# YOCO trunk, one core: four classical chunks at each half step's entry, mixing in three steps, a written order at the recurrence's end, squares moved to other engines

## Chip, cores and metric

One NeuronCore of a Trainium2 chip runs the whole program in one launch. The metric is device microseconds (us) of an execution; the lower the better. Traces come from the hardware profiler.

## The reference, cut to what matters

512 tokens, width 1024, two layers, everything in float32. Each layer does a half-step SwiGLU, a token mixer, a second half-step SwiGLU and a gated input embedding (PLE); layer 0 mixes by an HGRN2 gated linear recurrence, layer 1 by latent attention (MLA).

```python
def _rmsnorm(x, g):
    x32 = x.astype(jnp.float32)
    y = x32 * lax.rsqrt(jnp.mean(x32 * x32, axis=-1, keepdims=True) + EPS)
    return (y * g.astype(jnp.float32)).astype(x.dtype)

def _swiglu(h, w_in, w_out):
    gate, up = jnp.split(h @ w_in, 2, axis=-1)
    return (jax.nn.silu(gate) * up) @ w_out
...
    for li in range(DEPTH):
        g = norm_gains[li]
        x = x + 0.5 * _swiglu(_rmsnorm(x, g[0]), ffn_w_in[li, 0], ffn_w_out[li, 0])
        h = _rmsnorm(x, g[1])
        ...
        x = x + 0.5 * _swiglu(_rmsnorm(x, g[2]), ffn_w_in[li, 1], ffn_w_out[li, 1])
        gate = jax.nn.sigmoid((_rmsnorm(x, g[3]) @ ple_w_gate[li]).astype(jnp.float32))
        x = x + (gate * (p[li] @ ple_w_in[li]).astype(jnp.float32)).astype(x.dtype)
```

There are thus four half steps, called here FFN0 to FFN3, with a hidden width of 2816, that is 22 chunks of 128.

## The kernel before, in words

The residual stays on chip, transposed: eight tiles `x[m]` of 128 features by 512 tokens. Every operand of a product is split into a high and a low part (`split`: ACT rounds, DVE subtracts), and each product is three matmuls: high*high, high*low, low*high. Weights come in tiles of 128x1024 (512 KB), loaded by SP; a tile is *cut* into `whi` (ACT) and `wlo` (DVE) before PE can use it.

A half step (`ffn`) treats its 22 chunks in groups of 6, 8 and 8. The first two chunks (`PLAIN`) are *classical*: gate and up each take one weight tile and 24 matmuls of 512 columns. The other chunks go in *pairs* by Strassen's scheme: seven products of 24 matmuls of 256 columns replace eight. A pair needs sums of weight tiles (one made by a DMA that adds, issued by POOL, others by DVE) and sums of activations. The latter are made at the entry by `mix`, for each of four pairs of `x` tiles: ACT scales two tiles (`be`, `bo`), DVE makes two halves of `ta`, POOL two halves of `tb`, and `ta` and `tb` are split. A pair's first product needs none of them, the second `ta` and the third `tb` of all four. After each group, `outward` multiplies by the second weight matrix; `post` then splits the finished `x[m]` for what follows and adds its square to a running sum (`Stats`), ACT squaring and POOL adding, the last one added by DVE.

The half step runs in *slots*, one weight tile each: `work(t)` issues the load of a later tile, cuts tile t+2 and sums tile t+3; `at(dt, fn, late)` files other work in front of that or behind it. Inside `manual_schedule` the engines named keep the written order; elsewhere a planner orders every engine's instructions from its own estimates. In `plain` the four classical slots each hold one whole `mix` (line 398). FFN0 differs: its first two chunks are computed while `x` is still arriving (`primed`, lines 1163 to 1205, in an order written out for SP and PE), and its four `mix` calls stand before the slots, in the planner's hands.

The recurrence (`hgrn`) goes over four pairs of heads. `recur` is a generator with ten stretches: dots of q and k (line 204), three steps of score matmuls (line 706) whose results DVE copies under masks into `D` (line 716) while DVE and POOL scale q and k, then smaller products, the product with v, a norm and a spread. The planner fills PE meanwhile with independent chains: for the last pair the gates of heads 4 to 7 and the first half of the output projection (`project(0)`). `project(1)` needs the last two heads.

Of the kernel before, what the change touches and what calls it, by code (L numbers as in the profile page):

```python
# [21 lines left out]
DFF = 2816  # L22
NF = DFF // P
GROUPS = [(0, 6), (6, 14), (14, 22)]
PLAIN = 2
HT = T // 2
A_HEADS = 8
B_HEADS = 16
# [28 lines left out]
def kernel(  # L57
# [56 lines left out]
    def soon(n):  # L114
        return tc.high_priority(offset=n)
# [57 lines left out]


    class Stats:
        def __init__(self, n):
            self.n, self.acc, self.seen = n, None, 0
# [65 lines left out]

    ONE, TWO = slice(0, HT), slice(HT, T)

    def mix(nx, i, res):
        col, xg = nx.cols[0], nx.xg[0]
        be, bo = slot("be", F32, "r"), slot("bo", F32, "r")
        for b, m in ((be, 2 * i), (bo, 2 * i + 1)):
            act.activation(b, x[m], AF.Copy, scale=gain(col, m))  # L250
        ta, tb = slot("ta", F32, "r"), slot("tb", F32, "r")
        dve.tensor_tensor(out=ta[:, ONE], in0=be[:, ONE], in1=be[:, TWO], op=ALU.subtract)
        dve.tensor_tensor(out=ta[:, TWO], in0=bo[:, TWO], in1=be[:, TWO], op=ALU.subtract)
        pool.tensor_tensor(out=tb[:, ONE], in0=ta[:, TWO], in1=be[:, ONE], op=ALU.add)
        pool.tensor_tensor(out=tb[:, TWO], in0=tb[:, ONE], in1=bo[:, ONE], op=ALU.subtract)  # L255
        sa, sb = split(ta), split(tb)
        e, o = xg[2 * i], xg[2 * i + 1]
        res.append([
            tuple(a[:, t] for a in part)
            for part, t in ((e, ONE), (sa, ONE), (sb, ONE), (o, ONE), (sa, TWO), (o, TWO), (sb, TWO))  # L260
        ])

    class Weight:

# [42 lines left out]
    def ffn(nx, post, rb=None, primed=(), aside=None, ready=None):  # L307
# [3 lines left out]
        for lo, hi in GROUPS:  # L311
            for f in range(lo, hi):
                if f < PLAIN:
                    if not primed:
# [68 lines left out]
            act.copy(p[0], g)  # L383
            low(p, g)

        def plain():
            xg = nx.xg[0]

            def chain_of(w):
                ps = mm_bank()  # L390
                full(ps, w, xg, range(KC), True, True)
                return ps

            def mixing(i):
                mix(nx, i, b)

            at(0, lambda: mixing(0), True)
            p0 = chain_of(turn())
            sums = nx.stats.sums()
            r = nx.stats.columns(sums)  # L400
            now[0] += 1
            at(0, lambda: mixing(1), True)
            p1 = chain_of(turn())
            pb = spread(r)
            now[0] += 1

            def first_gate():
                st["rb"] = slot("rb", F32, "b")
                act.copy(st["rb"], pb)
                st["g"] = gated(p0)  # L410

            at(0, first_gate)
            at(0, lambda: kept(p1, st["g"]), True)
            if ready is not None:
                at(0, lambda: ready(st["rb"]), True)
            at(0, lambda: mixing(2), True)
            p2 = chain_of(turn())
            now[0] += 1

            def second_gate():  # L420
                st["g"] = gated(p2)

            at(0, second_gate)
            at(0, lambda: mixing(3), True)
            p3 = chain_of(turn())
            now[0] += 1
            at(0, lambda: kept(p3, st["g"]))

        def pair(last):
            g = qpool.tile([P, 2 * T], F32, tag="qq", bufs=2, name=name("g"))  # L430
# [106 lines left out]
            hidden.clear()  # L537

        if primed:
            for i in range(KC // 2):  # L540
                mix(nx, i, b)
            for f in range(PLAIN):
# [4 lines left out]
        with tc.manual_schedule(engines=ALL):  # L547
            for lo, hi in GROUPS:
                fs = range(lo, hi)
                if lo == 0 and not primed:  # L550
                    plain()
# [11 lines left out]
        stream["n"] = (stream["tiles"] - 2) * WB  # L563

    class Next:
        def __init__(self, cols, stats=True):
            self.cols = cols
            self.xg = [[] for _ in cols]
            self.stats = Stats(KC)

        def __call__(self, m):
            for i, col in enumerate(self.cols):
                self.xg[i].append(split(x[m], gain(col, m)))
            self.stats.add(x[m])

    def gcol(layer, i):
        return V_GAIN + (layer * 4 + i) * KC
# [18 lines left out]
    def hgrn(xg, stats, lower, upper, post):  # L596
# [75 lines left out]
        def recur(res, f, k, q, decay, v):  # L672
# [124 lines left out]
            dve.tensor_tensor(out=o1, in0=o1, in1=spread(r), op=ALU.mult)  # L797
            res.append(o1)

        def gate(h):  # L800
            pg = chain(xg)
# [9 lines left out]
            )  # L811
            outs[h] = split(o1, None, "o")

        def project(half):
            for m in range(KC):
                po = chain(outs[4 * half : 4 * half + 4])
                with soon(EV_OFF):
                    dve.tensor_tensor(out=x[m], in0=po, in1=x[m], op=ALU.add)
                    if half == 1:
                        post(m)  # L820

        pairs = A_HEADS // 2
        vals = values(0)
# [2 lines left out]
        for p in range(pairs):  # L826
            res = [[], []]
            live = [recur(res[e], *fkq[e], vals[e]) for e in range(2)]
            while live:
                live = [g for g in live if next(g, live) is not live]  # L830
            if p < pairs - 1:
                vals = values(p + 1)
                fkq = [keys(2 * p + 2 + e) for e in range(2)]
# [4 lines left out]
            if p == pairs - 1:  # L838
                sg = [gate(2 * p + e) for e in range(2)]
                project(0)  # L840
                for e in range(2):
                    finish(2 * p + e, *res[e], sg[e])
        project(1)


    def embed(layer):
# [313 lines left out]
            project(B_HEADS // 2 - 1, part)  # L1160


    first = Next([gcol(0, 0)])
    primed, heads = [mm_bank() for _ in range(4)], []

    def prime(c, *ks):
        for k in ks:
            w = tuple(a[:, k * P : (k + 1) * P] for a in heads[c])
            mm3(primed[c], w, first.xg[0][k], k == 0, k == KC - 1)

    def head(pieces=1):
        fetch(pieces)
        heads.append(stream["ready"].pop(0))
        stream["n"] += WB

    with tc.manual_schedule(engines={mybir.EngineType.SP, mybir.EngineType.PE}):
        nc.sync.dma_start(vc, vec)
        load(0)
        first(0)
        head(4)  # L1180
        prime(0, 0)
        for m in range(1, KC):
            load(m)
            first(m)
            if m == 2:
                head(2)
                prime(0, 1, 2)
                prime(1, 0, 1, 2)
            if m == 4:
                head(2)  # L1190
                for c in range(2):
                    prime(c, 3, 4)
                prime(2, *range(5))
            if m == 5:
# [5 lines left out]
        sums = first.stats.sums()  # L1200
        for c in range(3):
            prime(c, KC - 1)
        head()
# [205 lines left out]
```

## Time and profile before

| | |
|---|---|
| median of three runs | 2227.64 us (2226.56 to 2228.78) |
| the profiled execution | 2227.43 us, of which the span from first to last instruction is 2225.7 us |
| PE busy | 2170.2 us (98%) |
| DVE busy | 1567.6 us (70%) |
| ACT, POOL busy | 986.5 us (44%), 368.0 us (17%) |
| mean granted clock of TensorE | 0.985 of 2.4 GHz |

Matmuls overlap, so that a row's mean duration is longer than the distance from one matmul to the next; distances are read from elapsed time over counts. PEld is the weight load in front of each matmul.

### The profile page before, as it was taken

To read this page: it belongs to the slowest core of one execution; us is meant where nothing else is said; L and a number is where in the kernel's file an instruction comes from. 1 tells how busy PE (TensorE), PEld (TensorE's weight loads), DVE (VectorE), ACT (ScalarE), POOL (GpSimd) and SP (SyncE) were. 2 spreads that over 40 slices of the span, in tenths; PEclk is the share of its full clock that TensorE was granted. 3 is DMA by queue.
4 is the path that set the end of the run, shared out by engine and by line. 5 is a ranking of instruction groups with operands and counts; after the bars stand their busy time and mean duration, and the time that the engine had idled before them with its cause. 6 is when DMAs were issued, how large, how long until landed. Compare 5 with 4: busy or idle time off the path is not lost.

```text
span 2225.7 us, 33449 instructions
## 1 busy us (share of the span) xinstructions
PE 2170.2 (98%) x13314; PEld 1949.5 (88%) x13314; DVE 1567.6 (70%) x2270; ACT 986.5 (44%) x1393; POOL 368.0 (17%) x463
## 2 busy tenths in 40 slices
PE   7999999999998999999989999999999989999998
PEld 6899998889877899998878989988888868999987
DVE  7777676778777676676767757767677776775765
ACT  6344353322335443354553434446454554343543
POOL 3000001555433000001110000022111130000011
PEclk9999999999998999999989999999999989999999
DMA  5555552211123565552334655423122215664631
GB/s 181 163 152 161 141 163 99 79 64 67 67 71 90 152 156 160 150 155 101 104 95 133 180 151 144 152 85 105 60 84 86 67 58 151 160 167 129 179 105 48
DMA packets 77836, 267.80 MB, mean 120 GB/s; under 512 B 9328, under 2 KB 11504, under 8 KB 77680
## 3 DMA queue, kind: packets, MB, share of 16 engines
q1 hardware_dynamic: 65296, 222.25, 29.9%
q0 software_dynamic: 11520, 41.95, 11.2%
q8 instruction: 105, 1.72, 0.3%
q10 hardware_dynamic: 864, 1.46, 0.2%
q14 instruction: 51, 0.42, 0.1%
HBM read 259.33 MB, written 2.10 MB: 117 GB/s over the span
## 4 chain that ended last, share of the span: by engine, by line
PE 88%; DVE 4%; issue 4%; ACT 2%; POOL 1%; DMA 0%; POOLq 0%; DVEq 0%; SPq 0%; ACTq 0%
PE aux L301 20%; PE mm L301 15%; PE mm L151 15%; PE mm L150 15%; PE mm L152 15%; PE aux L706 1%; PE aux L151 1%; PE aux L152 1%; PE aux L150 1%; DVE wlo L292 1%; PE aux L1116 1%; POOL tb L255 1%; PE aux L1090 0%; PE aux L1091 0%; DVE wlo L129 0%
## 5 line engine op out<-in xcount | busy, mean ns | idle before, releaser
L151 PE MATMUL mm<-lo,whi 128*128 128x512 f32 x1544 | 609.4, 395 | 10.0 <-DVE lo L169 8.8
L150 PE MATMUL mm<-hi,whi 128*128 128x512 f32 x1544 | 604.3, 395 | 12.6 <-ACT whi L128 6.8
L152 PE MATMUL mm<-hi,wlo 128*128 128x512 f32 x1544 | 605.3, 392 | 0.5 <-DVE wlo L129 0.5
L292 DVE TENSOR_TENSOR wlo<-raw,whi 128x1024 fp32r<-128x1024 f32 x348 | 439.8, 1264 | 204.0 <-ACT whi L291 200.6
L291 ACT CAST whi<-raw 128x1024 fp32r<-128x1024 f32 x348 | 363.4, 1045 | 287.1 <-PE mm L151 151.2
L301 PE MATMUL aux<-hi,whi 128*128 128x256 f32 x1280 | 370.7, 290 | 12.7 <-ACT whi L291 5.3
L301 PE MATMUL aux<-lo,whi 128*128 128x256 f32 x1280 | 368.4, 288 | 4.5 <-DVE lo L166 4.5
L301 PE MATMUL aux<-hi,wlo 128*128 128x256 f32 x1280 | 368.3, 288 | 2.3 <-DVE wlo L292 2.0
L151 PEld LDWEIGHTS mm<-lo,whi 128*128 128x128 f32 x1544 | 292.1, 189 | 74.3 <-DVE lo L169 14.9
L150 PEld LDWEIGHTS mm<-hi,whi 128*128 128x128 f32 x1544 | 291.7, 189 | 73.8 <-ACT whi L128 6.8
L152 PEld LDWEIGHTS mm<-hi,wlo 128*128 128x128 f32 x1544 | 292.2, 189 | 59.0 <-DVE wlo L129 0.9
L301 PE MATMUL mm<-hi,whi 128*128 128x256 f32 x960 | 271.7, 283 | 0.0
L301 PE MATMUL mm<-lo,whi 128*128 128x256 f32 x960 | 271.7, 283 | 0.0
L301 PE MATMUL mm<-hi,wlo 128*128 128x256 f32 x960 | 271.6, 283 | 0.0
L301 PEld LDWEIGHTS aux<-hi,whi 128*128 128x128 f32 x1280 | 250.9, 196 | 15.5 <-ACT whi L291 6.0
L301 PEld LDWEIGHTS aux<-lo,whi 128*128 128x128 f32 x1280 | 251.3, 196 | 6.2 <-DVE lo L166 5.8
L301 PEld LDWEIGHTS aux<-hi,wlo 128*128 128x128 f32 x1280 | 251.0, 196 | 3.8 <-DVE wlo L292 2.7
L275 POOL DMA_DIRECT2D raw<-in_wall x80 | 69.7, 872 | 976.5 <-DMA raw<-in_wall 423.1
L301 PEld LDWEIGHTS mm<-hi,whi 128*128 128x128 f32 x960 | 184.4, 192 | 0.0
L301 PEld LDWEIGHTS mm<-lo,whi 128*128 128x128 f32 x960 | 184.4, 192 | 0.0
L301 PEld LDWEIGHTS mm<-hi,wlo 128*128 128x128 f32 x960 | 184.3, 192 | 0.0
L128 ACT CAST whi<-raw 128x1024 fp32r<-128x1024 f32 (+2 forms) x104 | 104.3, 1008 | 178.3 <-PE mm L151 131.6
(242 smaller groups left out, 2938.7 us busy)
## 6 DMA issues: line engine op xcount, KB each, us to landing
raw<-in_wall SPq DMA_DIRECT2D x407, 512.0 KB, 3.6
raw<-in_wall POOLq DMA_DIRECT2D x80, 512.0 KB, 6.2
x<-in_xT SPq DMA_DIRECT2D x8, 256.0 KB, 5.7
qr<-hi SPq DMA_DIRECT2D x32, 64.0 KB, 2.0
qr<-lo SPq DMA_DIRECT2D x32, 64.0 KB, 2.0
out_dram<-o SPq DMA_DIRECT2D x8, 256.0 KB, 2.4
p<-in_pT ACTq DMA_DIRECT2D x4, 256.0 KB, 5.1
cs<-in_cst SPq DMA_DIRECT2D x1, 385.0 KB, 7.1
```

The costliest lines, as they stand in the source:

```text
L128: act.copy(hi[:, s], raw[:, s])
L150: pe.matmul(out, a[0], b[0], start=first, stop=False)
L151: pe.matmul(out, a[0], b[1], start=False, stop=False)
L152: pe.matmul(out, a[1], b[0], start=False, stop=last)
L255: pool.tensor_tensor(out=tb[:, TWO], in0=tb[:, ONE], in1=bo[:, ONE], op=ALU.subtract)
L275: nc.gpsimd.dma_start(self.raw, wall[self.plus], accum_op=ALU.add)
L291: act.copy(hi, self.raw)
L292: dve.tensor_tensor(out=lo, in0=self.raw, in1=hi.bitcast(F32), op=ALU.subtract)
L301: pe.matmul(o, w[u][:, s], b[i][v], start=first and e + i + n == 0, stop=False, skip_group_check=True)
L706: pe.matmul(sc[:, e * 192 : (e + 1) * 192].rearrange("p (i b n) -> p i b n", i=2, n=3 * m), k[:, j * P : (j + 1) * P], q4[:, :, j * nbt : ...
L1116: pe.transpose(banks[b][:, o : o + P], prob[i][:, j * P : (j + 1) * P], ident)
```

## The change

`PLAIN` becomes 4: chunks 2 and 3 are now classical in every half step, which takes one pair from each. `mix` becomes a class with three steps: `scale` (ACT), `combine` (DVE, POOL) and `cut` (the splits). In FFN1 to FFN3 `plain` has eight slots: for tile pair i, `scale` in slot max(2i-1, 0), `combine` in slot 2i, `cut` in slot 2i+1. In FFN0 the two primed chunks stay, and four classical slots follow that hold one step of each kind.

At the recurrence's end, PE's order is written: after each stretch of each of the last two heads, `fill` steps (of three matmuls) of a generator that holds gates 4 to 7 and the first half of the projection. FFN0's sum of squares is made by PE (fp32 matmuls with a column of ones) in place of POOL and of the transposes; the sums in front of FFN1 and FFN3 are added by DVE in place of POOL.

```diff
-PLAIN = 2
+PLAIN = 4
+FILL = (3, 4, 3, 3, 3, 3, 3, 2, 2, 3)
...
-                eng = dve if self.seen == self.n else pool
+                eng = dve if self.seen == self.n else self.eng
...
+    class Mix:
+        def scale(self):
+            col = self.nx.cols[0]
+            self.be, self.bo = slot("be", F32, "r"), slot("bo", F32, "r")
+            for b, m in ((self.be, 2 * self.i), (self.bo, 2 * self.i + 1)):
+                act.activation(b, x[m], AF.Copy, scale=gain(col, m))
+        def combine(self):
...
+            dve.tensor_tensor(out=ta[:, TWO], in0=bo[:, TWO], in1=be[:, TWO], op=ALU.subtract)
+            dve.tensor_tensor(out=ta[:, ONE], in0=be[:, ONE], in1=be[:, TWO], op=ALU.subtract)
+            pool.tensor_tensor(out=tb[:, ONE], in0=ta[:, TWO], in1=be[:, ONE], op=ALU.add)
+            pool.tensor_tensor(out=tb[:, TWO], in0=tb[:, ONE], in1=bo[:, ONE], op=ALU.subtract)
+        def cut(self, res):
+            sa, sb = split(self.ta), split(self.tb)
...
+        def plain(f0):
+            mixed = [Mix(nx, i) for i in range(KC // 2)]
+            n = 2 * (PLAIN - f0)
+            if f0:
+                for i in range(KC // 2):
+                    if i == 0:
+                        mixed[0].scale()
+                        mixed[0].combine()
+                        mixed[0].cut(b)
+                        mixed[1].scale()
+                    else:
+                        at(i - 1, mixed[i].combine)
+                        at(i, lambda i=i: mixed[i].cut(b), True)
+                        if i < KC // 2 - 1:
+                            at(i - 1, mixed[i + 1].scale, True)
+            else:
+                for i in range(KC // 2):
+                    at(max(2 * i - 1, 0), mixed[i].scale, i > 0)
+                    at(2 * i, mixed[i].combine, i == 0)
+                    at(2 * i + 1, lambda i=i: mixed[i].cut(b), True)
...
+                ps[t] = aux_bank() if f0 and t < 2 else mm_bank()
+                full(ps[t], w, xg, range(KC), True, True)
...
+        def closing(done, sg):
+            last = 2 * (pairs - 1)
+            for e in range(4):
+                g = gated((yield from steps(xg)))
+                if e < 2:
+                    finish(last - 2 + e, *done[e], g)
+                else:
+                    sg.append(g)
+            for m in range(KC):
+                po = yield from steps(outs[0:4])
...
+        with tc.manual_schedule(engines={mybir.EngineType.PE}):
+            sg = []
+            rest = closing(done, sg)
+            for fill in FILL:
+                for g in live:
+                    next(g, None)
+                    for _ in range(fill):
+                        next(rest, None)
...
-    first = Next([gcol(0, 0)])
+    first = Next([gcol(0, 0)], None)
+    def square(m):
+        sq = slot("sq", F32, "r")
+        act.activation(sq, x[m], AF.Square)
+        for j in range(NT):
+            pe.matmul(
+                dots[:, j : j + 1], sq[:, j * P : (j + 1) * P], ones, start=m + j == 0, stop=m == KC - 1,
...
-    n2 = Next([gcol(0, 2)])
+    n2 = Next([gcol(0, 2)], dve)
-    n6 = Next([gcol(1, 2)])
+    n6 = Next([gcol(1, 2)], dve)
```

## Rows read from the trace of the kernel before

**Rows 1.** The page: busy time by engine, and the chain that ended last by engine.
```profile
PE 2170.2 (98%) x13314; PEld 1949.5 (88%) x13314; DVE 1567.6 (70%) x2270; ACT 986.5 (44%) x1393; POOL 368.0 (17%) x463
...
PE 88%; DVE 4%; issue 4%; ACT 2%; POOL 1%; DMA 0%; POOLq 0%; DVEq 0%; SPq 0%; ACTq 0%
```
**Rows 2.** Busy time by stretch: first the second pair of FFN0, then the first pair of FFN0 (without the two matmuls that ran ahead), FFN1, FFN2 and FFN3. Columns: stretch, its length, PE, PEld, DVE, ACT and POOL busy (with counts), granted clock, DMA share, GB/s.
```profile
64.62:84.83 20.21, 20.21 (x170) 20.21 (x169) 15.74 (x17) 10.72 (x14) 0.00 (x0) 1.00 0.49 159
38.00:64.62 26.62, 22.74 (x168) 22.34 (x167) 20.89 (x26) 14.87 (x19) 4.07 (x5) 0.87 0.55 143
698.70:729.17 30.47, 25.22 (x170) 23.75 (x168) 18.69 (x22) 14.71 (x19) 4.44 (x5) 0.83 0.47 122
1127.84:1159.89 32.05, 25.81 (x169) 24.15 (x168) 20.06 (x25) 15.32 (x20) 5.28 (x6) 0.79 0.46 114
1826.21:1854.87 28.66, 24.50 (x170) 23.25 (x169) 18.26 (x21) 14.10 (x19) 3.47 (x4) 0.88 0.49 129
```
**Rows 3.** The same view: two classical slots of FFN2 (48 matmuls of 512 columns), and four slots of an outward product (96 of them).
```profile
1116.83:1127.84 11.01, 11.01 (x51) 9.10 (x50) 6.95 (x9) 5.83 (x8) 2.27 (x3) 1.00 0.38 88
1011.95:1033.71 21.76, 21.76 (x98) 18.02 (x97) 14.98 (x17) 9.88 (x14) 5.17 (x4) 1.00 0.29 98
```
**Rows 4.** PE's waits from 1110 to 1152 us (FFN2's entry): who waited for what, us in total, times, longest.
```profile
PE aux L301 <- ACT whi L291: 3.7, 1, 3.7
...
PE aux L221 <- POOL t L197: 1.1, 1, 1.1
```
**Rows 5.** Timeline of FFN2's entry around its third `mix` (matmuls left out): start, duration, engine, line.
```profile
1125.63 0.72 ACT L250 ACTIVATE be<-x,vc 128x512 f32<-128x512 f32 x1
...
1128.16 0.42 DVE L252 TENSOR_TENSOR ta<-be 128x256 f32<-128x256 f32 x1
...
1128.99 0.74 POOL L254 TENSOR_TENSOR tb<-ta,be 128x256 f32<-128x256 f32 x1 [9.81 <-DVE ta L253]
...
1129.81 1.08 POOL L255 TENSOR_TENSOR tb<-tb,bo 128x256 f32<-128x256 f32 x1
1130.92 0.62 ACT L165 CAST hi<-tb 128x512 fp32r<-128x512 f32 x1 [1.36 <-POOL tb L255]
1131.57 0.69 DVE L166 TENSOR_TENSOR lo<-tb,hi 128x512 fp32r<-128x512 f32 x1 [1.28 <-ACT hi L165]
...
1133.50 1.03 ACT L291 CAST whi<-raw 128x1024 fp32r<-128x1024 f32 x1
...
1134.56 1.23 DVE L292 TENSOR_TENSOR wlo<-raw,whi 128x1024 fp32r<-128x1024 f32 x1 [1.69 <-ACT whi L291]
```
**Rows 6.** Busy time by stretch at the recurrence's end (columns as in rows 2): before the last pair's dots, from there to the second half of the projection, and the part with the three score steps.
```profile
576.70:597.90 21.20, 21.20 (x109) 17.84 (x108) 13.90 (x21) 7.79 (x13) 6.51 (x7) 1.00 0.21 75
597.90:654.40 56.50, 53.42 (x286) 45.71 (x284) 44.82 (x104) 14.12 (x23) 17.15 (x27) 1.00 0.22 66
599.00:626.00 27.00, 27.00 (x137) 23.48 (x138) 25.57 (x69) 5.39 (x6) 8.06 (x12) 1.00 0.17 59
```
**Rows 7.** Timeline, single instructions there: q*k of the last pair on POOL, its dots on PE, and PE's start on the second half of the projection.
```profile
580.75 2.59 POOL L674 TENSOR_TENSOR D<-q,k 128x512 f32<-128x512 f32 x2 [0.61 <-PE aux L151]
...
597.92 1.84 PE L204 MATMUL aux<-ones,D 128*128 128x1 f32 x16
...
654.39 1.20 PE L150 MATMUL mm<-hi,whi 128*128 128x512 f32 x4 [1.30 <-ACT hi L165]
```
**Rows 8.** Groups by line there: PE's score matmuls from 597.9 to 650 us, DVE's masked copies and residual additions from 599 to 626 us. Columns: count, busy us, mean ns, idle before.
```profile
L706 PE MATMUL aux<-qq,k 128*128 128x192 f32 x48 | 8.9, 327 | 0.0
...
L716 DVE COPY_PREDICATED D<-mk,aux 128x192 f32<-128x192 int32 (+2 forms) x36 | 10.6, 354 | 1.1 <-PE aux L706 1.0
...
L818 DVE TENSOR_TENSOR x<-mm,x 128x512 f32<-128x512 f32 x4 | 2.7, 683 | 0.0
```
**Rows 9.** The start: busy time of 6.85 to 32.2 us (columns as in rows 2), and single instructions in it.
```profile
6.85:32.20 25.35, 22.10 (x80) 15.69 (x81) 18.87 (x24) 16.57 (x30) 13.03 (x11) 0.93 0.64 224
...
12.31 3.05 POOL L187 TENSOR_TENSOR sq<-sq,sq 128x512 f32<-128x512 f32 x2 [0.34 <-ACT sq L182]
...
14.14 3.46 DVE L169 SCALAR_TENSOR_TENSOR lo<-x,vc,hi 128x512 fp32r<-128x512 f32 x2
...
15.96 0.50 PE L151 MATMUL mm<-lo,whi 128*128 128x512 f32 x1 [1.28 <-DVE lo L169]
```
**Rows 10.** Busy time by stretch (columns as in rows 2) where the mixers hand over: 60 matmuls of 512 columns and four transposes, from the last head of MLA to the end of FFN3's first chain; and 96 matmuls, from the second half of the recurrence's projection to the end of FFN1's first chain.
```profile
1785.32:1809.28 23.96, 18.90 (x64) 13.48 (x65) 21.11 (x24) 14.66 (x23) 12.60 (x8) 0.79 0.14 44
654.39:680.07 25.68, 23.58 (x96) 17.80 (x97) 22.47 (x26) 15.17 (x23) 9.89 (x6) 0.99 0.20 67
```
**Rows 11.** Groups by line from 1789 to 1803 us (columns as in rows 8), and, from the timeline, one split of `x` and one addition of squares on DVE at moments when POOL adds nothing.
```profile
L187 POOL TENSOR_TENSOR sq<-sq,sq 128x512 f32<-128x512 f32 x6 | 10.4, 1740 | 18.5 <-ACT sq L182 18.2
...
L169 DVE SCALAR_TENSOR_TENSOR lo<-x,vc,hi 128x512 fp32r<-128x512 f32 x5 | 5.6, 1120 | 0.0
...
L292 DVE TENSOR_TENSOR wlo<-raw,whi 128x1024 fp32r<-128x1024 f32 x2 | 4.0, 1976 | 0.0
...
L252 DVE TENSOR_TENSOR ta<-be 128x256 f32<-128x256 f32 x1 | 1.5, 1498 | 0.0
...
1789.43 0.74 DVE L169 SCALAR_TENSOR_TENSOR lo<-x,vc,hi 128x512 fp32r<-128x512 f32 x1
...
679.11 0.68 DVE L187 TENSOR_TENSOR sq<-sq,sq 128x512 f32<-128x512 f32 x1
```

More of the change, by code (lines that the diff above doesn't have):

```diff
@@ L244, with __init__ @@
     ONE, TWO = slice(0, HT), slice(HT, T)
[L246 to L261, printed above, removed]
+    class Mix:
+        def __init__(self, nx, i):
+            self.nx, self.i = nx, i
+        def scale(self):
[4 more added lines that the diff above has]
+        def combine(self):
+            be, bo = self.be, self.bo
+            ta, tb = self.ta, self.tb = slot("ta", F32, "r"), slot("tb", F32, "r")
+            dve.tensor_tensor(out=ta[:, TWO], in0=bo[:, TWO], in1=be[:, TWO], op=ALU.subtract)
[4 more added lines that the diff above has]
+            sa, sb = split(self.ta), split(self.tb)
+            xg = self.nx.xg[0]
+            e, o = xg[2 * self.i], xg[2 * self.i + 1]
+            res.append([
+                tuple(a[:, t] for a in part)
+                for part, t in ((e, ONE), (sa, ONE), (sb, ONE), (o, ONE), (sa, TWO), (o, TWO), (sb, TWO))
+            ])
     class Weight:
@@ L384, in kept, with fresh @@
             low(p, g)
-        def plain():
+        def plain(f0):
             xg = nx.xg[0]
[L389 to L407, printed above, removed]
+            mixed = [Mix(nx, i) for i in range(KC // 2)]
[17 more added lines that the diff above has]
+                    at(2 * i + 1, lambda i=i: mixed[i].cut(b), True)
+            ps = [None] * n
+            r = pb = None
+            def fresh():
@@ L424, in plain @@
[L424 to L427, printed above, removed]
+            for t in range(n):
+                f = f0 + t // 2
+                if t == 2 and not f0:
+                    at(0, fresh)
+                if t % 2 == 0 and t > 0:
+                    at(0, lambda t=t: st.update(g=gated(ps[t - 2])))
+                    at(0, lambda t=t: kept(ps[t - 1], st["g"]), True)
+                if t == 2 and not f0 and ready is not None:
+                    at(0, lambda: ready(st["rb"]), True)
+                w = turn()
+                ps[t] = aux_bank() if f0 and t < 2 else mm_bank()
+                full(ps[t], w, xg, range(KC), True, True)
+                if t == 0 and not f0:
+                    r = nx.stats.columns(nx.stats.sums())
+                if t == 1 and not f0:
+                    pb = spread(r)
+                now[0] += 1
@@ L539, in ffn @@
         if primed:
-            for i in range(KC // 2):
-                mix(nx, i, b)
-            for f in range(PLAIN):
+            for f in range(len(primed) // 2):
                 kept(primed[2 * f + 1], gated(primed[2 * f]))
@@ L549, in ffn @@
                 fs = range(lo, hi)
-                if lo == 0 and not primed:
-                    plain()
+                if lo == 0:
+                    plain(len(primed) // 2)
                 for f in fs:
@@ L798, in recur, with steps, gated @@
             res.append(o1)
+        def steps(rhs):
+            ps = mm_bank()
+            for k in range(len(rhs)):
+                mm3(ps, block(), rhs[k], k == 0, k == len(rhs) - 1)
+                yield
+            return ps
+        def closing(done, sg):
[8 more added lines that the diff above has]
+                po = yield from steps(outs[0:4])
+                with soon(EV_OFF):
+                    dve.tensor_tensor(out=x[m], in0=po, in1=x[m], op=ALU.add)
         def gate(h):
-            pg = chain(xg)
+            return gated(chain(xg))
+        def gated(pg):
             with soon(EV_OFF):
@@ L828, in hgrn @@
             live = [recur(res[e], *fkq[e], vals[e]) for e in range(2)]
+            if p == pairs - 1:
+                break
             while live:
                 live = [g for g in live if next(g, live) is not live]
-            if p < pairs - 1:
-                vals = values(p + 1)
-                fkq = [keys(2 * p + 2 + e) for e in range(2)]
+            vals = values(p + 1)
+            fkq = [keys(2 * p + 2 + e) for e in range(2)]
             if done is not None:
@@ L837, in hgrn @@
             done = res
[L838 to L843, printed above, removed]
+        with tc.manual_schedule(engines={mybir.EngineType.PE}):
[6 more added lines that the diff above has]
+                        next(rest, None)
+            for _ in rest:
+                pass
+            for e in range(2):
+                finish(2 * p + e, *res[e], sg[e])
+            project()
     def embed(layer):
@@ L1176 @@
     with tc.manual_schedule(engines={mybir.EngineType.SP, mybir.EngineType.PE}):
+        dots = aux_bank()
         nc.sync.dma_start(vc, vec)
@@ L1184 @@
             first(m)
+            if m == 1:
+                square(1)
             if m == 2:
@@ L1193 @@
                 prime(2, *range(5))
+            if m in (2, 4):
+                for k in (m - 1, m) if m == 4 else (m,):
+                    square(k)
             if m == 5:
@@ L1199 @@
                         prime(c, m)
-        sums = first.stats.sums()
+                square(m)
+        sums = dots[:, 0:NT]
         for c in range(3):
```

36 lines of the change are left out of this document (15 added, 21 removed).

## The prediction

> **What bounds the kernel now.** I read the page first. PE is busy 98% of the span and carries 88% of the chain that ended last [rows 1], so time can go in two ways alone: PE gets less to do, or it stands less and keeps its clock. Busy shares hide the second, since a matmul at half clock counts as busy. So next I read busy time by stretch, with elapsed time over the number of matmuls. A quiet pair takes 20.21 us at granted clock 1.00; the first pair of each half step takes 26.62, 30.47, 32.05 and 28.66 us at clock 0.87, 0.83, 0.79 and 0.88, a mean between the two levels of 2.4 and 1.2 GHz [rows 2]. That is the largest loss in the trace: 6.4 + 10.3 + 11.8 + 8.5 = 37.0 us. Of FFN2's, the waits name a weight cut (ACT whi), 3.7 us [rows 4], but the timeline shows that ACT is only the last in a queue: one `mix` walks from ACT (1125.63) over DVE (1128.16), POOL (1128.99 to 1130.89), ACT (1130.92) to DVE (1131.57), each engine standing for the other, and the cut filed behind it comes at 1133.50 [rows 5]. From `be` to the last split are 6.6 us, a classical slot lasts 5.5 [rows 3], so four whole mixes cannot fit four slots, and the pair's second and third product need them all.
>
> **The change part by part.**
>
> *Classical chunks.* Four slots of 24 matmuls take 21.76 us [rows 3]; the pair they replace takes 20.21 [rows 2]. Four half steps: 4 x 1.55 = +6.2 us. This is certain, since PE is the bound.
>
> *Mixing over eight slots.* Work per tile pair does not change, but has 43.5 us in place of 21.8. More than that, no engine meets its own half-made `mix`: `combine` waits for a `scale` filed a slot earlier, `cut` for a `combine` filed a slot earlier, and 5.5 us exceeds every such step (POOL's two additions end 2.7 us after DVE began [rows 5]). What is late next would be the gating of the last classical chunk in front of the first pair; it holds one weight cut of 1.03 + 1.23 us [rows 5], while the products that need that cut lie two slots ahead. FFN0 has four slots, but its first mix stands in front of them and each step again has a slot to itself; in those 21.8 us DVE has four cuts and what is left of four mixes, where it was busy 20.89 of 26.62 us before [rows 2]. I take the loss of the first pairs as gone up to 0.5 us each: -37.0 + 2 = -35.0 us. Bounds: -37.0, and -17 if half the queue remains. In FFN2 PE also waits 1.1 us for the norm's power on POOL [rows 4], behind the whole first mix; with its splits moved out I take -1 (bounds -1.1 and 0).
>
> *Written order at the recurrence's end.* Nothing is added or removed on PE. From the dots to the second half of the projection PE stands 56.50 - 53.42 = 3.1 us [rows 6], 1.3 of it at the end for the last split [rows 7]; the written order keeps nine steps of filling (9 x 3 x 0.227 = 6.1 us) behind the last spread, so these 3.1 go. Against it: gates can no longer run ahead of the dots. Before, PE had no idle time from 576.7 to 597.9 [rows 6], while POOL made the last pair's q*k only from 580.75 on, done by 583.3 [rows 7]; in the written order PE may stand for it, between 0 and 583.3 - 576.7 = 6.6 us. The pair before still has its own products in that time, so I take 0.6. And DVE: the three score steps hold 25.57 us of DVE work [rows 6]; PE is now given 20 filling steps there, 13.6 us, and the score matmuls, 8.9 us at most [rows 8], 22.5 together. DVE's residual additions, 2.7 us [rows 8], move out, since the gates now come first: 25.57 - 2.7 - 22.5 = 0.4 us; with both steps not overlapping well I take 1.5. Sum -3.1 + 0.6 + 1.5 = -1 us; bounds -3.1 and +8 (the 6.6, 3.5 of DVE and a little clock).
>
> *Squares of FFN0 on PE.* 32 dots make 64 matmul records; 16 take 1.84 us [rows 7], so +7.4 us of PE. Part falls where PE stands: 3.25 us of the first 25.35, at clock 0.93 [rows 9]. And POOL's additions go: two splits of `x` beside them took 3.46 us [rows 9] against 0.74 each alone [rows 11], and PE waited for just these at 15.96 [rows 9]. I take +2; bounds -2 (stalls and half clock gone as well) and +7.4 (no cover).
>
> *Squares in front of FFN1 and FFN3 on DVE.* At both places DVE is PE's releaser and is busy 21 to 22 of 24 to 26 us; PE loses there 23.96 - 60 x 0.227 - 0.4 = 9.9 and 25.68 - 96 x 0.227 = 3.9 us [rows 10]. Six additions of 0.68 put 4.1 us on DVE per place. What it gets back is read from the same stretch: beside POOL's six additions a split takes 1.12 in place of 0.74 (five: 1.9 us), a weight cut 1.98 in place of 1.23 (two: 1.5), and half a `ta` 1.50 in place of 0.42 (1.1) [rows 5, 11]; 4.5 us. So nearly even: I take -1 for both places, bounds +8.2 (nothing given back) and -10 (rival B).
>
> The Trainium skill (SBUF — State Buffer, section "Who interferes with whom") says that a DVE instruction with two SBUF inputs and a GpSimd instruction that reads SBUF exclude each other for a whole instruction. The stretched splits and cuts agree with it [rows 11]. By that rule POOL's six additions close the port for their own length, and the exchange gives more than even: that is rival B, whose price below stands on rows.
>
> The sum: +6.2 - 35.0 - 1 - 1 + 2 - 1 = -29.8 us on the profiled execution's 2227.43, which lies 0.2 under the median: **2197.6 us**.
>
> **The rivals.**
>
> *A. The written order starves PE mildly.* DVE's work in the score steps does not shrink and q*k comes late: +8 in place of -1, so 2206.6. For it: DVE at 25.57 of 27 us [rows 6]. Against: before, that load lay beside 27 us without idle time on PE, and half the region has little for DVE.
>
> *B. DVE is freed at the handovers.* POOL's six additions last 10.4 us in FFN3's handover [rows 11]; if DVE's work on two operands may lie beside none of them, 10.4 us come free for 4.1 paid, 6.3, and at FFN1's handover all of the 3.9 that PE loses there: -10 in place of -1, so 2188.6. For it: splits are what PE waits for. Against: the additions now stand in DVE's own queue in front of the next split.
>
> *C. Half the first pairs' loss stays,* since the queue in front of the pair is also gating and weight cuts: +18, so 2215.6. For it: the wait names whi [rows 4]. Against: second pairs, with as many cuts, lose nothing [rows 2].
>
> *D, the other side.* The written order serialises PE and DVE: at each of the 20 places PE waits for the head's whole share. A head's score step is 25.57 / 6 = 4.3 us of DVE; six of them are 25.6 us, the other 14 places at the 1.3 us of the last split [rows 7] 18 more, and with PE working half the time the clock falls as in FFN2's first pair, which costs its region another 20% (15 us). Together +59, against -29 for the rest: about 2258. It decides from 30 us lost in that region, that is, when PE stands a third of it. For it: PE's queue is fixed, and one late DVE copy holds everything behind it. Against: the fill between two stretches of one head (4.1 to 5.4 us and the other head's matmuls) is longer than 4.3 us.
>
> **How the numbers follow.** Chances: my forecast (2190 to 2204) 0.52, A 0.18, B 0.16, C 0.08, D 0.04, and 0.02 for a disorder of the planner elsewhere. The range goes from B's far end to C's: 2182 to 2214 us. A measurement of this kernel can tell 0.2%, 4.5 us, from no change; faster means below 2223. Forecast, A, B and C lie there; with a little taken off for several mishaps at once: faster 0.93, same 0.02, slower 0.05.
>
> **What would show it.** First pairs at 20 to 21 us and clock 1.00 in all four half steps prove the mixing; a wait of PE in the first pair on anything from `Mix` refutes it. Eight slots at 43.5 us prove the price of the classical chunks. Recurrence: PE's idle time between the last pair's dots and the projection under 3 us, and DVE near full in the score steps. Start: FFN0's first slot about 2 us later than prime's end at 38.0 was before. Handovers: splits of `x` back at 0.74 us, and PE's loss in the two stretches of rows 10 near 13 us in all; near 5 would be B. I am wrong if the sum comes right by other terms, or if the first pairs are clean and the time is still above 2214.

## The result and the profile after

The changed kernel takes 2199.58 us (median of four, 2199.11 to 2200.0), the kernel before on the same chip 2227.29; the ratio is 0.9875, 95% interval 0.9858 to 0.9892. The prediction was 2197.6. The sum came out, but two of its terms were wrong by 7 and by 4 us, in opposite directions, so that it came within 2 us is in part luck. One execution of a kernel below (`e2_gates_first`) took 12208 us, with every matmul more than five times as long, and is left out.

The page after, the lines of [rows 1]:

```profile
PE 2166.1 (99%) x13086; PEld 1938.7 (88%) x13086; DVE 1522.0 (69%) x2252; ACT 968.6 (44%) x1373; POOL 330.0 (15%) x437
...
PE 94%; DVE 3%; issue 1%; ACT 1%; DMA 0%; POOL 0%; POOLq 0%; SPq 0%; DVEq 0%; ACTq 0%
```

PE's share of the chain rose from 88 to 94%: it still bounds the kernel and stands less. Busy time by stretch (columns as in [rows 2]): from the start to FFN0's first slot, FFN0's four slots, the first pairs of FFN0 to FFN3, and the eight slots of FFN1, FFN2 and FFN3.

```profile
6.85:41.00 34.15, 34.15 (x164) 29.32 (x165) 15.26 (x24) 18.15 (x31) 3.10 (x4) 1.00 0.58 201
41.00:62.78 21.78, 21.78 (x98) 18.02 (x97) 18.84 (x27) 13.85 (x22) 7.92 (x8) 1.00 0.36 96
62.78:82.93 20.15, 20.15 (x170) 20.15 (x168) 12.83 (x14) 10.80 (x13) 0.00 (x0) 1.00 0.46 153
722.76:742.91 20.15, 20.15 (x169) 20.14 (x168) 12.38 (x13) 10.72 (x13) 0.00 (x0) 1.00 0.44 141
1141.60:1161.75 20.15, 20.15 (x169) 20.15 (x168) 12.38 (x13) 10.73 (x13) 0.00 (x0) 1.00 0.44 143
1826.57:1846.73 20.16, 20.16 (x170) 20.15 (x169) 12.38 (x13) 10.74 (x13) 0.00 (x0) 1.00 0.41 143
...
679.22:722.76 43.54, 43.54 (x197) 36.03 (x196) 28.51 (x41) 24.06 (x35) 9.94 (x11) 1.00 0.37 103
1098.06:1141.60 43.54, 43.54 (x197) 36.04 (x196) 28.42 (x42) 22.86 (x34) 9.00 (x11) 1.00 0.37 104
1783.03:1826.57 43.54, 41.91 (x181) 34.24 (x182) 27.63 (x39) 20.56 (x30) 10.46 (x11) 0.96 0.37 104
```

All four first pairs last 20.15 us at clock 1.00, where [rows 2] had 26.62 to 32.05. FFN3's slots are cut as the last 43.54 us before its pair; the last of the handover's stall lies in that stretch.

The rest of the time is read from the *ways* between half steps: from the last pair of one to the first pair of the next, less the classical slots at their own length (21.76 before, 43.54 after). The same view, before (FFN0 to FFN1, FFN1 to FFN2, FFN2 to FFN3):

```profile
323.80:698.70 374.90, 369.72 (x2003) 319.21 (x2002) 279.59 (x532) 128.23 (x199) 156.07 (x230) 1.00 0.23 76
988.40:1127.84 139.44, 138.30 (x618) 114.04 (x617) 94.19 (x113) 70.08 (x99) 24.15 (x20) 1.00 0.31 99
1421.39:1826.21 404.82, 396.01 (x2038) 335.64 (x2037) 288.14 (x576) 200.69 (x368) 80.04 (x97) 0.98 0.25 80
```

and after:

```profile
321.88:722.76 400.88, 395.02 (x2098) 340.70 (x2097) 290.06 (x556) 138.95 (x214) 148.78 (x226) 0.98 0.23 77
981.88:1141.60 159.72, 159.72 (x714) 132.23 (x713) 107.61 (x134) 80.67 (x115) 25.65 (x24) 1.00 0.31 101
1402.97:1826.57 423.60, 416.05 (x2134) 352.41 (x2133) 299.97 (x600) 210.08 (x382) 71.11 (x93) 0.99 0.26 82
```

FFN0 to FFN1, with the recurrence and a handover: 353.1 before, 357.3 after, +4.2. FFN1 to FFN2: 117.7 and 116.2, -1.5. FFN2 to FFN3: 383.1 and 380.1, -3.0. So the one loss lies on the way with the recurrence. There, by stretch:

```profile
576.00:598.00 22.00, 17.48 (x76) 14.72 (x75) 8.67 (x18) 3.50 (x7) 5.97 (x6) 0.69 0.06 24
598.00:626.00 28.00, 27.30 (x143) 23.06 (x142) 26.24 (x73) 6.53 (x9) 12.62 (x20) 1.00 0.18 58
```

PE stands 4.5 of 22 us and its clock falls to 0.69. These 22 us lie *in front of* the score steps; the score steps themselves, with DVE 26.24 of 28 us busy, lose 0.7. The timeline says who held whom (start, duration, engine, line; first PE, then POOL and DVE):

```profile
579.81 0.39 PE L152 MATMUL aux<-al,vhi 128*128 128x256 f32 x1 [0.92 <-DVE al L798]
...
581.37 0.65 PE L214 MATMUL aux<-cs,sq 128*128 128x128 f32 x4 [0.77 <-ACT sq L183]
...
585.17 1.12 PE L222 MATMUL aux<-cs,t 128*128 128x128 f32 x4 [2.71 <-POOL t L198]
586.08 1.71 PE L205 MATMUL aux<-ones,D 128*128 128x1 f32 x8
...
588.22 0.63 PE L152 MATMUL mm<-lo,whi 128*128 128x512 f32 x1
588.64 0.63 PE L153 MATMUL mm<-hi,wlo 128*128 128x512 f32 x1
```
```profile
581.51 2.49 POOL L691 TENSOR_TENSOR D<-q,k 128x512 f32<-128x512 f32 x2
584.11 1.01 POOL L198 TENSOR_TENSOR t<-t,mhalf 128x4 f32<-128x4 f32 x1
...
583.26 0.77 DVE L195 TENSOR_SCALAR t<-t 128x4 f32<-128x4 f32 x1
```

PE is at the tail of the *earlier* pair: its last products, its norm and its spread. The written order puts nothing in front of that tail, because every gate now stands behind the *next* pair's dots. So PE waits for its links in turn, for a split by DVE (0.92 us), for a square by ACT (0.77) and for the norm's power (2.71); the dots behind it wait for nothing. After that a matmul of 512 columns comes every 0.43 us (588.22 to 596.3) in place of 0.23: the lower of the two levels, 1.2 GHz.

The power in the longest wait comes behind the next pair's two q*k in POOL's queue. They cost little of it: its operand comes from DVE at 583.26 + 0.77 = 584.03 us, just when the q*k end. From the norm's first transpose (L214, 581.37) to the spread (585.17) pass 3.8 us, in which PE has nothing to do.

### The profile page after: what moved, and what is told of

Read it like the earlier page. It is cut to its first block, busy times and chain, and to the rows that moved or that the text cites. A ratio compares the mean times of both kernels' runs of the same rounds, so it can differ in the third digit from the quotient of the medians.

```text
span 2197.3 us, 32868 instructions
## 1 busy us (share of the span) xinstructions
PE 2166.1 (99%) x13086; PEld 1938.7 (88%) x13086; DVE 1522.0 (69%) x2252; ACT 968.6 (44%) x1373; POOL 330.0 (15%) x437
## 4 chain that ended last, share of the span: by engine, by line
PE 94%; DVE 3%; issue 1%; ACT 1%; DMA 0%; POOL 0%; POOLq 0%; SPq 0%; DVEq 0%; ACTq 0%
PE aux L314 19%; PE mm L151 17%; PE mm L152 17%; PE mm L153 17%; PE mm L314 14%; PE aux L152 2%; PE aux L153 2%; PE aux L151 1%; PE aux L723 1%; PE aux L1162 1%; PE aux L1136 0%; PE aux L1137 0%; DVE wlo L130 0%; PE aux L1221 0%; PE aux L214 0%
## 5 line engine op out<-in xcount | busy, mean ns | idle before, releaser
L151 PE MATMUL mm<-hi,whi 128*128 128x512 f32 x1656 | 651.1, 395 | 11.2 <-ACT whi L129 6.8
L152 PE MATMUL mm<-lo,whi 128*128 128x512 f32 x1656 | 651.3, 393 | 5.2 <-DVE lo L170 3.7
L153 PE MATMUL mm<-hi,wlo 128*128 128x512 f32 x1656 | 649.0, 392 | 0.0
L314 PE MATMUL aux<-hi,whi 128*128 128x256 f32 x1152 | 327.4, 284 | 0.0
L314 PE MATMUL aux<-hi,wlo 128*128 128x256 f32 x1152 | 325.9, 283 | 0.0
L314 PE MATMUL aux<-lo,whi 128*128 128x256 f32 x1152 | 325.9, 283 | 0.0
L314 PE MATMUL mm<-hi,whi 128*128 128x256 f32 x864 | 244.5, 283 | 0.0
L314 PEld LDWEIGHTS aux<-hi,whi 128*128 128x128 f32 x1152 | 220.8, 192 | 0.6
L314 PEld LDWEIGHTS aux<-lo,whi 128*128 128x128 f32 x1152 | 220.9, 192 | 0.5
L314 PEld LDWEIGHTS aux<-hi,wlo 128*128 128x128 f32 x1152 | 220.9, 192 | 0.0
```

Of the source, the lines that this page charges most:

```text
L151: pe.matmul(out, a[0], b[0], start=first, stop=False)
L152: pe.matmul(out, a[0], b[1], start=False, stop=False)
L153: pe.matmul(out, a[1], b[0], start=False, stop=last)
L314: pe.matmul(o, w[u][:, s], b[i][v], start=first and e + i + n == 0, stop=False, skip_group_check=True)
```

## The experiments

All edits are to the changed kernel. The kernel before, run anew beside these, took 2224.82, 2225.84 or 2227.76 us; so times are compared by ratio, and stretches by the ways defined above.

**The planner's order again** (`e1_planner_order`, at the recurrence's end alone):

```diff
-        with tc.manual_schedule(engines={mybir.EngineType.PE}):
-            rest = closing(done, sg)
...
-            for fill in FILL:
...
+        sg = [gate(2 * p + e) for e in range(2)]
+        ...
+        project()
```

> The changed kernel with the recurrence's end left to the planner again; all else as changed. In the changed kernel PE stands from 578.6 to 585.2 us in front of the written order and then runs at half clock, 10.9 us lost between 575 and 600. My theory: the written order keeps gates 4 to 7 behind the last pair's dots, so that nothing fills the end of the pair before. Then this kernel loses little there, and pays the 3 to 4 us in front of the projection's second half again: about 2192.5 us (7 less than 2199.6). Rival: the loss is the earlier pair's own and stays, while the written order's gain at the end goes: about 2203 us.

2192.14 us against 2224.82, ratio 0.9853 (0.9839 to 0.9868), as the theory had it. By stretch, its way from FFN0 to FFN1, the place of the stall, and the recurrence's last part:

```profile
321.64:716.36 394.72, 391.22 (x2098) 338.11 (x2097) 291.79 (x556) 138.43 (x214) 148.01 (x226) 0.99 0.25 78
...
572.00:598.00 26.00, 26.00 (x140) 22.21 (x139) 18.28 (x30) 9.11 (x16) 6.74 (x8) 1.00 0.23 77
...
626.00:655.00 29.00, 26.00 (x127) 21.40 (x126) 18.37 (x35) 8.63 (x16) 6.71 (x12) 0.93 0.16 54
```

The way is 394.72 - 43.54 = 351.2, 6.2 less than with the written order: there is no stall before 598, and the 3 us in front of the projection, which the written order was to remove, are back. The written order as it stands costs 6 us net.

**The written order, fed** (`e2_gates_first`; `e8_gates_again` is the same kernel once more, for a profile): ten steps of gates go ahead of the first stretch.

```diff
-FILL = (3, 4, 3, 3, 3, 3, 3, 2, 2, 3)
+AHEAD = 10
+FILL = (1, 4, 3, 3, 2, 2, 2, 2, 2, 3)
...
+            for _ in range(AHEAD):
+                next(rest, None)
```

> The written order stays, but ten filling steps (gate 4 and a quarter of gate 5, 6.8 us of PE) stand in front of the last pair's first stretch, and the later stretches get ten fewer. My theory: the end of the pair before is covered, TensorE's granted clock stays 1.00 there, and about 10 of the 10.9 us come back: 2189.6 us. Rival: with less filling in the score steps DVE binds there (it is busy 26.2 of 28 us from 598 to 626 in the changed kernel), and half is given back: 2195 us.

> The same kernel as e2_gates_first (ten steps of gates, copies and projection put ahead of the written score steps), for a profile of it. Theory, the written order's loss is the wait for the earlier pair's tail: TensorE now has about 10 us of other matmuls in front of that wait, so the 10.9 us lost between 575 and 600 us falls below 3 us and the granted clock stays at 1.00 there, FFN0's last pair to FFN1's first slot takes about 349.5 to 351 (after: 357.34), the time is 2192 to 2194. Rival, the half clock goes with the short score steps themselves: the stretch of the first score steps still stands below 0.85 and the loss stays above 6 us.

e2: ratio 0.9862 (0.9846 to 0.9879); e8: 2195.22 us in one run. e8's way and the stretches at the recurrence's end:

```profile
322.45:717.37 394.92, 392.22 (x2098) 339.08 (x2097) 291.71 (x556) 138.58 (x214) 149.03 (x226) 0.99 0.25 78
...
576.00:598.00 22.00, 19.94 (x99) 17.37 (x98) 14.26 (x24) 5.55 (x11) 6.52 (x7) 0.84 0.14 49
...
626.00:655.00 29.00, 28.36 (x140) 23.33 (x139) 19.89 (x33) 10.89 (x19) 2.97 (x5) 1.00 0.21 72
```

The way is 351.4, as with the planner. So the cause of the 6 us is shown: without filling in front of the earlier pair's tail PE stands. e2's time is what its rival gave (2194.55 against 2195), but not for the rival's reason: from 598 to 626 us PE of e8 is busy 28.00 of 28 us, so DVE doesn't bind there. And e8's own expectation held only in part. PE still stood 2.06 of the 22 us and the clock was 0.84, not 1.00, as the rival said (below 0.85; its loss of over 6 us was too much). What the written order saves in the last stretch (28.36 of 29 us busy against 26.00) it pays here. Whether the wait of 1.8 us or the short matmuls around it brought the clock down isn't settled.

That wait also tells what q*k is worth. In e8 POOL did it from 579.44 us on and stood idle before the power, and PE waited for that power all the same (POOL, then PE):

```profile
588.61 1.01 POOL L199 TENSOR_TENSOR t<-t,mhalf 128x4 f32<-128x4 f32 x1 [1.44 <-DVE t L196]
...
589.67 0.65 PE L223 MATMUL aux<-cs,t 128*128 128x128 f32 x4 [1.79 <-POOL t L199]
```

From the norm's transposes (586.37) to the spread pass 3.3 us, against 3.8 with q*k in between. So the wait is the norm's own way over DVE and POOL, and q*k put at most some 0.5 us on it.

**Room or steps?** The mix got both, eight slots and three steps. `e3_whole_mix` keeps the slots and puts all three steps of a mix into one; `e4_four_slots` keeps the steps and gives FFN1 to FFN3 two classical chunks again, with the mix filed as FFN0's four slots have it (the first one whole, in front of them).

```diff
# e3
-                    at(max(2 * i - 1, 0), mixed[i].scale, i > 0)
-                    at(2 * i, mixed[i].combine, i == 0)
-                    at(2 * i + 1, lambda i=i: mixed[i].cut(b), True)
+                    at(2 * i, mixed[i].scale, True)
+                    at(2 * i, mixed[i].combine, True)
+                    at(2 * i, lambda i=i: mixed[i].cut(b), True)
# e4
+        PLAIN = 4 if primed else 2
...
-            if f0:
+            if n == 4:
...
```

> Eight classical slots stay in FFN1 to FFN3, but each mix is whole again (scale, combine and cut one behind the other), in slots 0, 2, 4 and 6. This tells room from steps. If room alone does it: 2199.6 within 1 us and first pairs at 20.15 us. My theory: mostly room; a whole mix of 6.6 us makes weight cuts late by 1 to 2 us in its slot, the next slot recovers: first pairs at 20 to 21 us, some tenths to 1 us lost in each half step, 2200 to 2203 us. If the steps are what counts: first pairs at 25 us or more, above 2212 us.

> FFN1 to FFN3 have two classical chunks again (four slots) but with the mix in three steps, filed as FFN0's four slots have it; FFN0 as changed. Three times 1.55 us less for PE. If the steps alone remove the stall: 2195 us and first pairs at 20.15 us. If room is needed as well (my theory: in four slots the steps overlap with the norm's sums, the first gating and the table load, which FFN0's slots do not have): a third to a half of the 30.6 us of these three first pairs comes back, 2205 to 2210 us.

e3: 2211.16 us in one run; e4: 2207.92, ratio 0.9924 (0.9908 to 0.9941). The first pairs of FFN1, FFN2 and FFN3, and the second part of MLA up to its last head's product, of e3:

```profile
722.43:743.14 20.71, 20.44 (x170) 20.23 (x169) 14.46 (x16) 10.68 (x13) 0.00 (x0) 1.00 0.45 151
1143.29:1167.81 24.52, 22.16 (x170) 21.75 (x168) 16.30 (x17) 11.81 (x15) 0.00 (x0) 0.93 0.41 129
1838.24:1858.97 20.73, 20.46 (x170) 20.25 (x168) 14.48 (x16) 10.69 (x13) 0.00 (x0) 1.00 0.45 151
...
1609.13:1776.99 167.86, 165.68 (x887) 140.40 (x885) 118.45 (x272) 78.63 (x158) 22.92 (x38) 1.00 0.24 74
```

the first pairs of e4:

```profile
702.39:724.10 21.71, 20.66 (x170) 20.26 (x168) 15.51 (x18) 10.69 (x13) 0.86 (x1) 1.00 0.49 135
1121.47:1145.95 24.48, 22.04 (x169) 21.52 (x168) 17.23 (x19) 10.68 (x13) 0.86 (x1) 0.93 0.47 126
1814.79:1835.00 20.21, 20.21 (x170) 20.21 (x169) 13.98 (x16) 10.72 (x13) 0.88 (x1) 1.00 0.56 149
```

and that part of MLA, after:

```profile
1602.97:1766.24 163.27, 163.07 (x888) 140.34 (x886) 116.88 (x272) 79.12 (x158) 22.32 (x38) 1.00 0.23 77
```

Neither alone does it, and FFN2 is where both are needed. With the slots but whole mixes, the first pairs lose 0.6 + 4.4 + 0.6 us; in FFN2's pair PE waits 2.1 us for an eviction by ACT (L465 of that kernel), which stands behind the gating of the last chunk, which stands behind the last mix. In FFN2's slots PE waits 1.2 us for the norm's power again. With the steps but four slots the pairs lose 1.6 + 4.3 + 0.1 us, in FFN2's again with 2.3 us for that eviction. Of the 30.6 us that the first pairs of FFN1 to FFN3 lost before, each alone thus gives back some 80%, both together all.

The way from FFN2 to FFN3 is 5.5 us longer too, in e3 (429.11 us against 423.60) as in e4 (407.36 - 21.76 - 380.1). But 4.6 of these lie in MLA, in front of FFN3's mixes: the same matmuls up to its last head take 167.86 us (e4: 167.84) in place of 163.27. The planner orders MLA; why it takes longer in both isn't shown, and it tells nothing of room or steps. e4's time lies in the range expected of it, though more of the pairs came back than a third to a half. e3 missed its range by 8 us, through FFN2's pair and MLA.

**Squares at the handovers on POOL again** (`e5_pool_squares` in the changed kernel, `e11_planner_pool` with the planner's order):

```diff
-    n2 = Next([gcol(0, 2)], dve)
+    n2 = Next([gcol(0, 2)])
-    n6 = Next([gcol(1, 2)], dve)
+    n6 = Next([gcol(1, 2)])
```

> The squares in front of FFN1 and FFN3 are added by POOL again; all else as changed. In the changed kernel POOL is idle at both handovers, splits of x take 0.74 us and weight cuts 1.22 us there, and the handovers are about 4 and 3 us shorter than before the change. If POOL's additions had been in DVE's way (rival B of the prediction): splits back at 1.0 us and more, and 5 to 7 us slower, 2206 us. If the exchange was even, as I forecast: 2200 us within 1.5 us.

> Planner order at the recurrence's end, and the squares at FFN1's and FFN3's entry added by GpSimd as before. Theory, GpSimd's work beside VectorE's splits is what lengthens the handover: FFN1's entry takes 2 to 3 us longer than in e1_planner_order (FFN0's end to FFN1's first slot 353 to 354.2, before had 353.1), FFN3's 3 us longer (383.1), the time is 2197 to 2198. Rival, GpSimd's squares cost at FFN3's entry alone, as after's own order showed (+0.2 and +3.2): then FFN0's end to FFN1's first slot stays at 351.2 to 351.6 and the time is 2195.5.

One run each, 2202.68 and 2194.29 us. Ways from FFN2 to FFN3, of e5 and e11:

```profile
1403.60:1830.36 426.76, 416.85 (x2134) 353.14 (x2133) 300.64 (x594) 210.24 (x382) 80.34 (x99) 0.99 0.27 82
```
```profile
1395.52:1821.53 426.01, 415.00 (x2135) 351.75 (x2133) 299.89 (x594) 209.80 (x382) 81.45 (x99) 0.99 0.27 82
```

The way to FFN3 is 3.2 us longer with POOL's squares (e5, 426.76 against 423.60) and 3.5 (e11, 426.01 against e1's 422.47). From FFN0 to FFN1 they cost nothing: 401.05 us in e5 against 400.88, and 394.05 in e11, 0.7 below e1. So e5 lies between its two marks, and e11 is what its rival said: the squares count at FFN3 alone.

The way to FFN3 also varies by 3 us between kernels with the same squares (e6 below), so the handover itself is the better witness. From the last product of MLA's last head (after: 1765.97 us) to FFN3's first pair, less the slots, it is 20.1 us before, 20.3 in e5 and 19.9 in e11, all with POOL's squares; with DVE's it is 17.1 after, in e1 and in e10, and 18.2 to 18.5 in e6, e8 and e9. So DVE's squares gain 1.4 to 3.2 us there. PE's waits in the handover, e5:

```profile
PE mm L152 <- DVE lo L170: 6.2, 4, 4.0
```

after:

```profile
PE mm L152 <- DVE lo L170: 3.7, 4, 2.8
```

2.5 us less waiting for splits. DVE's groups there, e5 (1768 to 1790 us) and after (1766 to 1790):

```profile
L170 DVE SCALAR_TENSOR_TENSOR lo<-x,vc,hi 128x512 fp32r<-128x512 f32 x8 | 8.5, 1090 | 0.0
...
L305 DVE TENSOR_TENSOR wlo<-raw,whi 128x1024 fp32r<-128x1024 f32 x2 | 4.4, 2200 | 0.1
```
```profile
L170 DVE SCALAR_TENSOR_TENSOR lo<-x,vc,hi 128x512 fp32r<-128x512 f32 x8 | 6.7, 856 | 0.0
...
L305 DVE TENSOR_TENSOR wlo<-raw,whi 128x1024 fp32r<-128x1024 f32 x3 | 3.7, 1217 | 0.0
```

Beside POOL's additions a weight cut takes 2200 ns in place of 1217, as in [rows 11]. So DVE is freed when they go, as rival B says; its price is another matter.

**FFN0's sum of squares** on DVE (`e6_first_dve`) and on POOL as before (`e7_first_pool`, with `Next([gcol(0, 0)])`), in place of PE; the diff is e6's:

```diff
-    first = Next([gcol(0, 0)], None)
+    first = Next([gcol(0, 0)], dve)
...
-        square(0)
...
-                square(m)
-        sums = dots[:, 0:NT]
+        sums = first.stats.sums()
```

> FFN0's squares are added by DVE, and summed by the four transposes as before, in place of the 64 matmul records on PE; all else as changed. PE is busy without a gap from 6.85 to 41.0 us in the changed kernel, DVE 15.3 of these 34 us. My theory: the dots cost PE what they last, less what stood before; DVE has room for 4.8 us of additions and POOL's are not in its way: the first slot starts 5 us earlier, 2194.6 us. Rival: the additions stand in DVE's queue in front of the splits that release PE: no gain, 2199 us or more.

> FFN0's squares are added by POOL and summed by transposes, as in the kernel before; all else as changed. The prediction's term was +2 us for taking them to PE, and the first slot now starts at 41.0 us against 38.0 for what stood there before: so 3 us faster, 2196.6 us, with PE waiting on splits of x as before. If the planner's other freedom in that stretch matters more (mixes no longer stand there), 2194 us.

e6: 2191.84 us, ratio 0.9844 (0.9828 to 0.9861); e7: 2194.82, one run. From the start to FFN0's first pair, after, e6 and e7:

```profile
6.85:62.78 55.93, 55.93 (x261) 47.35 (x262) 34.10 (x50) 32.00 (x52) 11.02 (x11) 1.00 0.50 160
```
```profile
6.85:54.01 47.16, 47.13 (x200) 37.32 (x201) 38.70 (x58) 32.03 (x52) 10.94 (x11) 1.00 0.58 191
```
```profile
6.85:58.96 52.11, 49.52 (x201) 38.31 (x201) 41.01 (x52) 31.95 (x52) 19.89 (x17) 0.97 0.55 172
```

On PE the squares leave it no idle time at all, and yet are the slowest of the three: without the 64 records of its dots e6 reaches the first pair 8.8 us earlier. With the squares on POOL PE stands 2.6 us and loses some clock, and is still 3.8 better than with its own dots. Two groups of 16 records, after:

```profile
8.25 3.40 PE L1221 MATMUL aux<-ones,sq 128*128 128x1 f32 x16
...
31.23 1.84 PE L1221 MATMUL aux<-ones,sq 128*128 128x1 f32 x16
```

The first group takes twice as long as the later one. PE is slow at the start: matmuls of 512 columns too come every 0.43 us or more there, until 16.4 us in the changed kernel, but only until 10.2 in e6 (the rows give 1.00 for the granted clock all the same). The five groups take 8.3 us of PE in all, and four transposes in e6 some 0.4; the rest of the 8.8 is the longer slow start.

In e6 the way from FFN2 to FFN3 is 3.2 us longer, 2.0 of them up to MLA's last head and 1.2 in the handover, so that its gain in the whole is less than 8.8.

**What beats both** (`e9_planner_dve`: e1 and e6; `e10_gates_dve`: e2 and e6; their diffs together).

> Planner order at the recurrence's end (e1_planner_order) and FFN0's squares added by VectorE (e6_first_dve) together. The two stretches are 250 us apart and share no buffer in use, so the gains should add: 0.9853 x 0.9844 / 0.9875 = 0.9822 of before, which is 2185 to 2188 by this chip's before; FFN0's first pair starts at about 54.0 and the way from FFN0's end to FFN1's first slot is 351.2. Rival, a start 8.8 us earlier is given back where the first layer waits for its loads: then the time stays at 0.984 and above.

> Gates first in the written order (e2_gates_first) and FFN0's squares added by VectorE (e6_first_dve) together. Adding: 0.9862 x 0.9844 / 0.9875 = 0.9831 of before, 2187 to 2190. If the written order, once fed, is the better one, it comes below the planner's order with the same squares; if its short score steps cost time of their own, it stays 1 to 3 us above.

e9: 2184.62 us, ratio 0.9809 (0.9794 to 0.9824). e10: 2186.01, ratio 0.9818 (0.9802 to 0.9835). The planner's order is 1.4 us ahead, less than these intervals can tell. The gains add, as the ratios foretold (0.9822 and 0.9831 lie within these intervals). e9 is 0.0066 of before, some 15 us, under the changed kernel, with the planner's order back and FFN0's squares on DVE.

## Why the prediction was right, and where it was not

*Classical chunks, +6.2:* right. Eight slots take 43.54 us.

*Mixing, -35.0:* right in place and mechanism, 2 us short; no residue was left, -37.2. Every pair is at clock 1.00 and PE waits for no step of `Mix`. That it takes both room and steps, argued from two rows (6.6 us of mix in a slot of 5.5), e3 and e4 show.

*FFN2's spread wait, -1:* measured -1.5 on the way, and e3, with the whole first mix in front of the power again, has 1.2 us of it back.

*Written order, -1:* wrong, +6 (e1 against after). The failed sentence is "The pair before still has its own products in that time, so I take 0.6". Those products were there, but they and the norm and spread behind them are a chain over DVE, ACT and POOL, and nothing was left to run while PE waits for it: 4.5 us of standing, and then half the clock until 596.7. The bound beside it (583.3 - 576.7 = 6.6 us, POOL's late q*k) is near the measured value by luck: no dot waited for q*k, and e8 shows that the spread's wait isn't q*k's either. The other half, DVE full in the score steps, cost 0.7 us where I took 1.5. The 3.1 us in front of the projection did go. The sign that I had named, PE's idle time between the dots and the projection, came out well and didn't see the loss, which lies in front of the dots. So the price is near rival A's, with neither of its two causes.

*FFN0's squares on PE, +2:* measured +3.0 (first slot at 41.0 in place of 38.0), of which the squares alone are 3.8 by e7, the rest of that stretch having gained a little. "Part falls where PE stands" was too kind: the 64 records take 8.3 us, more than the +7.4, since 16 of them came while PE was slow. That DVE would do better still, by 5 us more than POOL (e6 against e7), I hadn't considered.

*Handovers, -1:* too small by 4. At FFN3 it is -3, the squares' doing (e5, e11), about half of rival B's 6.3. What PE gains isn't all that DVE is freed of, but what of it PE waited for, and 2.8 of the 3.7 us left are for a split behind a weight cut, the first mix's `combine` and an addition of squares on DVE (1780.94 to 1783.35 us). The Trainium skill (SBUF — State Buffer, section "Who interferes with whom") says that a DVE instruction with two SBUF inputs and a GpSimd instruction that reads SBUF contend. The 2200 ns against 1217 agree with that. PE's loss at the two handovers is 9.9 - 3.0 = 6.9 us and 0.6, between the two marks I gave (13 and, for rival B, 5). At FFN1 the way, with the recurrence's 6 taken off, is about 2 shorter, and the squares have no part in it: from the last spread to FFN1's first slot e5 and after both take 30.2 us, and with the planner's order it is 21.8 in e11, 22.5 in e1 and 24.5 before. Before, DVE's cut of a weight tile stood between the last two splits; the timeline of DVE there, in the kernel before:

```profile
676.63 1.90 DVE L292 TENSOR_TENSOR wlo<-raw,whi 128x1024 fp32r<-128x1024 f32 x1 [0.33 <-ACT whi L291]
678.45 0.74 DVE L169 SCALAR_TENSOR_TENSOR lo<-x,vc,hi 128x512 fp32r<-128x512 f32 x1
```

In e5 and e11, with POOL's squares too, the cuts fall elsewhere: none stands right in front of the last split. That the longer classical part moved them there is argued from the traces; no run has tried it alone.

So +6.2 - 37.2 - 1.5 + 4.2 (way with the recurrence and FFN1's handover) + 3.0 - 3.0 = -28.3, and the two executions differ by 2227.43 - 2199.11 = 28.3. The largest term was right by its mechanism. That the total is only 2 us off is luck: 7 us too little for the written order and 1 for the squares on PE met 4 too few at the handovers and 2 at the mixing.

## What to carry to other kernels

When an engine's order is written out by hand, list for every instruction that waits what independent work stands *in front of* it, from the place where the order begins and with the earlier iteration's tail included; what stands behind it can't fill. Half-made work that walks over several engines wants each step filed a slot after the one that feeds it, and enough slots: room or steps alone gave back some 80% of the first pairs' loss here, and FFN2 needed both. Work put on the bounding engine to fill its waits is paid in full when those waits are gone, as the dots show.

## What the runs showed of the hardware

A stall cost more than its length. PE stood 4.5 of 22 us, and matmuls of 512 columns then came every 0.43 us until 596.7, with a granted clock of 0.69 over the stretch; even with 2.06 us of standing it was 0.84. A weight cut on DVE beside POOL's additions took 2200 ns in place of 1217, a split 1090 in place of 856. And matmuls of one column are dear: 8 records took 0.81 us and 16 took 1.70 from their start to the next matmul's, 0.10 us each, against 0.23 between matmuls of 512 columns; 16 at the slow start took 3.27.
